# Keys of two inputs from one moving operand, and attention tiles in the halves of the context rows

## The chip, the cores and the metric

The kernel runs on one core of a Trainium2 chip. The metric is device time in microseconds of one execution; the median of three runs of the kernel before is 1750.83 us (1750.73 to 1752.44). A profiled execution on the same chip gives the trace.

## What is computed

One layer of a block over 256 latent tokens and 256 context tokens of width 2048, all in float32. Both inputs are normalized and modulated; the latent one goes through one large input projection, the context only through its key and value columns. Three branches follow: a convolution of 31 taps, a gating unit with a layer norm and a mixing matmul over tokens, and an attention of 16 heads whose keys are the latent tokens of a window and all of the context. The branches are gated, summed and projected, and a squared-ReLU MLP of width 8192 ends the layer.

```python
hl = modulate(rms_norm(xl, norm1_g[l]), mod_l[0], mod_l[1])
hc = modulate(rms_norm(xc, norm1_g[l]), mod_c[0], mod_c[1])
zl = hl @ w_in[l] + b_in[l]
zkv = hc @ w_in[l, :, K_OFF:G_OFF] + b_in[l, K_OFF:G_OFF]
kc, vc = split_heads(zkv[..., :NA_DIM]), split_heads(zkv[..., NA_DIM:])
y_na_l = neighbourhood_attention(q, k, v, kc, vc, na_rpb[l])
xl = xl + mod_l[2][:, None, :] * mixer_output(zl, y_na_l, *branch_params)
hl2 = modulate(rms_norm(xl, norm2_g[l]), mod_l[3], mod_l[4])
xl = xl + mod_l[5][:, None, :] * sq_relu_ffn(hl2, w_ff1[l], b_ff1[l], w_ff2[l], b_ff2[l])
```

## The kernel before

Every float32 product is made of three: a value is split into a high part (`hi`) and the rest (`lo`), and hi x hi, hi x lo and lo x hi are summed in PSUM. Weights come in as `raw` tiles of 128 x 1024 on the SP queue (ring of 8); ScalarE casts each to `whi` (L102) and VectorE subtracts to get `wlo` (L105), each in a ring of four, so that a `wlo` of a step can be written only when TensorE is done with the one four steps earlier. One such tile feeds about twelve matmuls. Rows of the inputs are transposed once and kept as `h`: 128 features by 512, the high parts of 256 tokens and then the low parts, two feature tiles in one unit of the shared pool, and each input has its own eight units (`hl[v][kt]`).

The shared pool (`unit`, `HEAP` = 27 units of 4 KB a partition) serves nearly all larger tiles of the program, one after another; a tile gets the slot of one whose last reader is done, and its first writer waits for that reader. A scheduler orders the instructions of each engine beforehand, from the order of the code and from when it takes slots and inputs to be ready; on the chip each engine runs its list in that order and waits where it must.

The stages: the modulation vectors and the first rows (to about 30 us); five blocks of keys and values over both inputs (to some 240 us), whose feature tiles are `BLOCKS`; the queries, and the attention beside the convolution's projections; the gating unit's projections (to about 540 us); three branch projections with their gates (to some 940 us); the output projection and the MLP.

Of these the change touches:

- the keys in `kv_block` (`kfn`): for each key tile `nt` and each input, `mm_w` runs per feature tile one matmul of 512 columns (L203, weight high part x rows high and low) and one of 256 (L205, weight low part x rows high, added onto the second half of the bank). The two halves of the bank are then joined and added to `kT`: in block 0 by an ACT step with the bias (L435) and a DVE add (L436), in the other blocks by an ACT copy (L438), a DVE add (L439) and a POOL add (L440), for each of the two inputs. The values `vb` (L212 to L215, `mm_x`) are added by one DVE step of 128 x 512 (L456).
- the attention: `qT` for queries (units of two tiles), `kh` and `kl` for the parts of a key tile (`att_keys`, L547 to L552), `oT` for the outputs (L617 and on) have units of their own; `S` (L583, L584) are scores, `pT` (L606) the transposed weights.
- by the pool, what comes later. The convolution reads its input `uT` with 248 steps on DVE, spread over the code (`conv_taps`, L689 and L692). The gating unit (`sgu_var`) squares its rows into a pool tile `svq` on ACT (L856), for the sum alone; then come L858 (DVE), L859 (POOL), `sgu_norm` (L862, L863 on DVE) and `sgu_mix`, eight pairs of matmuls (L871). Beside them the first branch runs with its gates (L897, L907). The steps of the modulation of later stages (L944, L946 on DVE, `mcol` L975) go between all of these.

## Time and profile before

| | us |
|---|---|
| median of three runs | 1750.83 |
| profiled execution | 1752.01 |
| its span | 1750.2 |
| PE busy | 1719.4 (98%) |
| DVE busy | 1333.6 (76%) |
| ACT busy | 874.6 (50%) |
| POOL busy | 127.3 (7%) |

PE is the engine of the matmuls, DVE VectorE, ACT ScalarE, POOL GpSimd. A busy time is the time in which at least one instruction runs; matmuls overlap at their ends, so that the distance of two starts tells what one costs, and its own duration is longer. The profile was taken from one execution, whose own time is 1.2 us above the median.

### The profile page before, as it was taken

How to read it: one execution, taken by the hardware profiler on the slowest of the kernel's cores; microseconds unless marked ns; L12 is line 12 of the kernel's file. 1: busy time of each engine (PE TensorE's matmuls, PEld its weight loads, DVE VectorE, ACT ScalarE, POOL GpSimd, SP SyncE). 2: the span in 40 equal slices, each digit the busy share in tenths (PEclk: the TensorE clock that was granted, in tenths of full speed). 3: DMA queues.
4: the chain of work that ended last, by engine and by line, in shares of the span. 5: the costliest groups of instructions: out<-in, count | busy, mean ns of one | idle time of the engine just before them, and what ended most of it. 6: DMA issues, size and time to landing. Idle time of an engine off the chain costs nothing.

```text
span 1750.2 us, 24238 instructions
## 1 busy us (share of the span) xinstructions
PE 1719.4 (98%) x8849; PEld 1426.7 (82%) x8849; DVE 1333.6 (76%) x2088; ACT 874.6 (50%) x1298; POOL 127.3 (7%) x179
## 2 busy tenths in 40 slices
PE   6999999999999999999999999999999999999997
PEld 4667878788888888788888888888888888888886
DVE  4655789799999987997889878756885576666665
ACT  4433427986545444564444565434543455335543
POOL 2222230110000010200000010000000000000000
PEclk9999999999999999999999999999999999999999
DMA  9898578657667778898898977867886776666552
GB/s 322 283 322 272 151 221 255 185 141 214 198 191 225 226 235 279 271 314 297 291 300 296 316 238 251 259 194 225 276 270 195 220 241 191 204 193 190 187 195 79
DMA packets 266969, 411.87 MB, mean 235 GB/s; under 512 B 13182, under 2 KB 128050, under 8 KB 266850
## 3 DMA queue, kind: packets, MB, share of 16 engines
q1 hardware_dynamic: 259410, 391.21, 68.9%
q0 software_dynamic: 6864, 18.07, 4.4%
q8 instruction: 69, 1.13, 0.3%
q10 hardware_dynamic: 576, 1.05, 0.2%
q14 instruction: 50, 0.41, 0.1%
HBM read 408.18 MB, written 2.10 MB: 234 GB/s over the span
## 4 chain that ended last, share of the span: by engine, by line
PE 79%; DVE 1%; ACT 1%; issue 0%; POOL 0%; POOLq 0%; DVEq 0%
PE bk L203 18%; PE bk L212 16%; PE bk L213 16%; PE bk L215 16%; PE bk L205 9%; PE o L617 1%; PE pT L606 1%; PE S L584 0%; PE S L583 0%; DVE wlo L105 0%; PE mrow L965 0%; PE mix L871 0%; PE mT L920 0%; ACT whi L102 0%; PE x1T L1138 0%
## 5 line engine op out<-in xcount | busy, mean ns | idle before, releaser
L102 ACT CAST whi<-raw 128x1024 fp32r<-128x1024 f32 x544 | 571.3, 1052 | 663.8 <-PE bk L213 430.3
L105 DVE TENSOR_TENSOR wlo<-raw,whi 128x1024 fp32r<-128x1024 f32 x544 | 670.3, 1234 | 285.2 <-ACT whi L102 274.9
L203 PE MATMUL bk<-h,whi 128*128 128x512 f32 x1536 | 395.1, 394 | 0.2 <-DVE h L1190 0.2
L203 PEld LDWEIGHTS bk<-h,whi 128*128 128x128 f32 x1536 | 273.8, 189 | 50.7 <-issue 2.7
L205 PEld LDWEIGHTS bk<-h,wlo 128*128 128x128 f32 x1536 | 216.0, 190 | 19.4
L205 PE MATMUL bk<-h,wlo 128*128 128x256 f32 x1536 | 221.7, 282 | 0.0
L213 PE MATMUL bk<-whi,g 128*128 128x512 f32 (+1 forms) x516 | 199.7, 387 | 0.0
L212 PE MATMUL bk<-whi,g 128*128 128x512 f32 (+1 forms) x516 | 199.7, 387 | 0.0
L946 DVE SCALAR_TENSOR_TENSOR ga<-raw,cst,ga 128x512 f32<-128x512 f32 x240 | 186.4, 777 | 2.1
L212 PE MATMUL bk<-whi,h 128*128 128x512 f32 x448 | 175.4, 392 | 0.0
L213 PE MATMUL bk<-whi,h 128*128 128x512 f32 x448 | 174.4, 389 | 0.0
L215 PE MATMUL bk<-wlo,g 128*128 128x512 f32 (+1 forms) x516 | 139.3, 387 | 0.0
L215 PE MATMUL bk<-wlo,h 128*128 128x512 f32 x448 | 122.2, 389 | 0.0
L212 PEld LDWEIGHTS bk<-whi,g 128*128 128x128 f32 x516 | 96.9, 188 | 19.7
L213 PEld LDWEIGHTS bk<-whi,g 128*128 128x128 f32 x516 | 96.9, 188 | 19.7
L215 PEld LDWEIGHTS bk<-wlo,g 128*128 128x128 f32 x516 | 96.5, 188 | 19.8
L692 DVE SCALAR_TENSOR_TENSOR cT<-uT,wcT,cT 128x249 f32<-128x249 f32 (+14 forms) x240 | 103.6, 476 | 0.6
L215 PEld LDWEIGHTS bk<-wlo,h 128*128 128x128 f32 x448 | 84.1, 188 | 17.5
L213 PEld LDWEIGHTS bk<-whi,h 128*128 128x128 f32 x448 | 84.1, 188 | 17.1
L212 PEld LDWEIGHTS bk<-whi,h 128*128 128x128 f32 x448 | 84.1, 188 | 17.0
L203 PE MATMUL k<-h,whi 128*128 128x512 f32 x256 | 69.2, 404 | 4.9 <-DVE t L439 2.5
L440 POOL TENSOR_TENSOR kT<-kT,t 128x256 f32<-128x256 f32 x64 | 52.6, 845 | 139.8 <-DVE t L439 139.5
(276 smaller groups left out, 1975.5 us busy)
## 6 DMA issues: line engine op xcount, KB each, us to landing
raw<-in_w_ff_dram SPq DMA_DIRECT2D x256, 512.0 KB, 4.4
raw<-in_w_in_dram SPq DMA_DIRECT2D x208, 512.0 KB, 4.7
raw<-in_w_mod_dram SPq DMA_DIRECT2D x192, 512.0 KB, 5.4
raw<-in_w_o_dram SPq DMA_DIRECT2D x32, 512.0 KB, 5.5
raw<-in_w_na_out_dram SPq DMA_DIRECT2D x16, 512.0 KB, 4.5
raw<-in_w_sgu_out_dram SPq DMA_DIRECT2D x16, 512.0 KB, 5.6
raw<-in_w_conv_out_dram SPq DMA_DIRECT2D x16, 512.0 KB, 5.4
bias<-in_na_rpb_dram POOLq DMA_DIRECT2D x16, 192.0 KB, 4.9
```

Source lines behind the costliest of these rows:

```text
L102: nc.scalar.copy(hv, rv)
L105: self.low[j] = nc.vector.tensor_tensor(lv, rv, hv.bitcast(F32), ALU.subtract)
L203: PE.matmul(bk, lhsT=hi[:, j, c0 : c0 + P], rhs=xhl, start=start, stop=False)
L205: PE.matmul(bk[:, T:], lhsT=lo[:, j, c0 : c0 + P], rhs=xhl[:, :T], start=False, stop=stop)
L212: PE.matmul(bk, lhsT=xhl[:, t * P : (t + 1) * P], rhs=hi, start=start, stop=False)
L213: PE.matmul(bk, lhsT=xhl[:, T + t * P : T + (t + 1) * P], rhs=hi, start=False, stop=False)
L215: last["mm"] = PE.matmul(bk, lhsT=xhl[:, t * P : (t + 1) * P], rhs=lo, start=False, stop=stop)
L440: GP.tensor_tensor(d, d, f, ALU.add)
L606: PE.transpose(b[:, kt * T + t * P : kt * T + (t + 1) * P], s[:, t, (2 * g + kt) * P : (2 * g + kt + 1) * P], ident)
L617: PE.matmul(b[64 * j : 64 * j + 64, :T], lhsT=vN[kt][:, h * 64 : h * 64 + 64], rhs=pts[j][:, kt], start=kt == 0, stop=kt == 3)
L692: V.scalar_tensor_tensor(a[:, lo:hi], u[:, lo + d : hi + d], wj, a[:, lo:hi], ALU.mult, ALU.add)
L946: V.scalar_tensor_tensor(a[0], raw[:, r], sc, a[0], ALU.mult, ALU.add)
```

## The change

The unit of a feature tile now holds both inputs: the latent rows in its first half, the context rows in its second (`hl[kt][:, v]`), sixteen units either way. In blocks 1 to 4 a key matmul reads the high parts of both inputs at once, or the low parts of both (`mm_both`): two pieces of 256 columns, one from each half. All three products go to the same bank, 256 columns for each input, and one DVE add of 128 x 512 brings it to `kT`. Block 0, where the two inputs come at different times, runs three matmuls of 256 columns per input (`mm_one`), and ACT adds the bias on the way to `kT`. Once the values have used the context rows, their halves take the queries and the attention outputs (`spare_half`, tiles 0 to 7) and the key parts (tiles 8 to 15, by turns); `qT`, `kh`, `kl` and `oT` need no units any more.

```diff
--- before.py
+++ after.py
@@ -303,7 +303,7 @@
 
     m1A = cp.tile([P, NK, 2], F32, name="m1A")
     m1B = cp.tile([P, NK, 2], F32, name="m1B")
-    hl = [[None] * NK, [None] * NK]
+    hl = [None] * NK
     kT = [None] * 8
     vN = [None] * 4
 
@@ -397,11 +397,9 @@
                     tps = aux("hT")
                     for t in range(2):
                         PE.transpose(tps[:, t * P : (t + 1) * P], nat[v][kt // 4][:, t, (kt % 4) * P : (kt % 4 + 1) * P], ident)
-                    if kt % 2 == 0:
-                        hl[v][kt] = unit([P, 2, 512], F32R, "h")
-                    else:
-                        hl[v][kt] = hl[v][kt - 1]
-                    dst = hl[v][kt][:, kt % 2]
+                    if hl[kt] is None:
+                        hl[kt] = unit([P, 2, 512], F32R, "h")
+                    dst = hl[kt][:, v]
                     sA, sB = m1A[:, kt, v : v + 1], m1B[:, kt, v : v + 1]
                     last["hi"] = S.activation(dst[:, :T], tps[:, :T], AF.Identity, bias=sB, scale=sA)
                     f = tmp(256, "hf")
@@ -411,7 +409,28 @@
         return steps, post
 
     def H(v, kt):
-        return hl[v][kt][:, kt % 2]
+        return hl[kt][:, v]
+
+    def spare_half(kt):
+
+        return hl[kt][:, 1]
+
+    def mm_both(b, hi, lo, c0, kts):
+
+        bv = b.rearrange("p (v t) -> p v t", v=2)
+        for j, kt in enumerate(kts):
+            PE.matmul(bv, lhsT=hi[:, j, c0 : c0 + P], rhs=hl[kt][:, :, :T], start=j == 0, stop=False)
+            PE.matmul(bv, lhsT=hi[:, j, c0 : c0 + P], rhs=hl[kt][:, :, T:], start=False, stop=False)
+        for j, kt in enumerate(kts):
+            PE.matmul(bv, lhsT=lo[:, j, c0 : c0 + P], rhs=hl[kt][:, :, :T], start=False, stop=j == len(kts) - 1)
+
+    def mm_one(todo):
+
+        for bk, hi, lo, j, c0, xhl, start, stop in todo:
+            PE.matmul(bk[:, :T], lhsT=hi[:, j, c0 : c0 + P], rhs=xhl[:, :T], start=start, stop=False)
+            PE.matmul(bk[:, :T], lhsT=hi[:, j, c0 : c0 + P], rhs=xhl[:, T:], start=False, stop=False)
+        for bk, hi, lo, j, c0, xhl, start, stop in todo:
+            PE.matmul(bk[:, :T], lhsT=lo[:, j, c0 : c0 + P], rhs=xhl[:, :T], start=False, stop=stop)
 
     def kv_block(bi):
         k0, nk = BLOCKS[bi]
@@ -421,23 +440,23 @@
         def kfn(p, vs=(0, 1)):
             def fn(*ws):
                 hi, lo = ws[0]
-                n = kc // P if bi == 0 and p == 0 and vs == (0,) else 1
+                if bi:
+                    for i in range(kc // P):
+                        nt = kc // P * p + i
+                        b = bank("k")
+                        mm_both(b, hi, lo, i * P, range(k0, k0 + nk))
+                        d = kT[nt][:, nt % 2]
+                        V.tensor_tensor(d, d, b, ALU.add)
+                    return
+                n = kc // P if p == 0 and vs == (0,) else 1
                 for i0 in range(0, kc // P, n):
                     bs = {(i, v): bank("k") for i in range(i0, i0 + n) for v in vs}
-                    mm_w([(b, hi, lo, j, i * P, H(v, k0 + j), j == 0, j == nk - 1) for (i, v), b in bs.items() for j in range(nk)])
+                    mm_one([(b, hi, lo, j, i * P, H(v, k0 + j), j == 0, j == nk - 1) for (i, v), b in bs.items() for j in range(nk)])
                     for (i, v), b in bs.items():
                         nt = kc // P * p + i
                         if kT[nt] is None:
                             kT[nt] = kT[nt ^ 1] = unit([P, 2, 512], name="kT")
-                        d = kT[nt][:, nt % 2, v * T : (v + 1) * T]
-                        f = tmp()
-                        if bi == 0:
-                            S.activation(f, b[:, T:], AF.Identity, bias=par["k"][:, nt : nt + 1])
-                            V.tensor_tensor(d, b[:, :T], f, ALU.add)
-                        else:
-                            S.copy(f, b[:, T:])
-                            V.tensor_tensor(f, b[:, :T], f, ALU.add)
-                            GP.tensor_tensor(d, d, f, ALU.add)
+                        S.activation(kT[nt][:, nt % 2, v * T : (v + 1) * T], b[:, :T], AF.Identity, bias=par["k"][:, nt : nt + 1])
             return fn
 
         def vfn(cb, vs=(0, 1)):
@@ -523,9 +542,7 @@
             V.scalar_tensor_tensor(g.rearrange("p (r c) -> p r c", c=64)[:, :, ::-1],
                                    b[:, :T].rearrange("p (r c) -> p r c", c=64), 0.125,
                                    f.rearrange("p (r c) -> p r c", c=64), ALU.mult, ALU.add)
-            if i == 0:
-                qT[nt] = qT[nt + 1] = unit([P, 2, 2, T], F32R, "qT")
-            q = qT[nt][:, i]
+            q = qT[nt] = spare_half(nt).rearrange("p (h t) -> p h t", h=2)
             up, dn = slice(0, 64), slice(64, P)
             S.copy(q[up, 0], g[up])
             S.copy(q[dn, 1], g[dn])
@@ -539,17 +556,18 @@
 
         bias_tile(nt)
         k = kT[nt][:, nt % 2]
-        hi = unit([P, 2, 512], F32R, "kh")
-        lo = unit([P, 2, 512], F32R, "kl")
+        at = 8 + 4 * (nt % 2)
+        hi = [spare_half(at + r) for r in range(2)]
+        lo = [spare_half(at + 2 + r) for r in range(2)]
         kW[nt] = hi, lo
         half = [slice(0, 64), slice(64, P)]
         for r in range(2):
-            S.copy(hi[half[r], r], k[half[r]])
-            S.copy(hi[half[1 - r], r], k[half[r]])
+            S.copy(hi[r][half[r]], k[half[r]])
+            S.copy(hi[r][half[1 - r]], k[half[r]])
         for r in range(2):
-            V.tensor_tensor(lo[half[r], r], k[half[r]], hi[half[r], r].bitcast(F32), ALU.subtract)
+            V.tensor_tensor(lo[r][half[r]], k[half[r]], hi[r][half[r]].bitcast(F32), ALU.subtract)
         for r in range(2):
-            S.copy(lo[half[1 - r], r], lo[half[r], r].bitcast(F32))
+            S.copy(lo[r][half[1 - r]], lo[r][half[r]].bitcast(F32))
 
     mask = cp.tile([P, 64], F32, name="mask")
     GP.memset(mask, 0.0)
@@ -579,9 +597,9 @@
         for t in range(2):
             b = aux("S")
             hi, lo = kW[nt]
-            q = qT[nt][:, nt % 2, h % 2, t * P : (t + 1) * P]
-            PE.matmul(b, lhsT=q, rhs=hi[:, h % 2], start=True, stop=False)
-            PE.matmul(b, lhsT=q, rhs=lo[:, h % 2], start=False, stop=True)
+            q = qT[nt][:, h % 2, t * P : (t + 1) * P]
+            PE.matmul(b, lhsT=q, rhs=hi[h % 2], start=True, stop=False)
+            PE.matmul(b, lhsT=q, rhs=lo[h % 2], start=False, stop=True)
             V.tensor_tensor_reduce(s[:, t, :T], b[:, :T], bt[nt][:, h % 2, (2 - 2 * t) * 64 : (6 - 2 * t) * 64],
                                    scale=-1.0, scalar=BIG, op0=ALU.add, op1=ALU.min, accum_out=mx[:, 2 * t : 2 * t + 1])
             V.tensor_tensor_reduce(s[:, t, T:], b[:, T:], zero, scale=-1.0, scalar=mx[:, 2 * t : 2 * t + 1],
@@ -615,9 +633,7 @@
             for j in range(2):
                 h = 2 * nt + j
                 PE.matmul(b[64 * j : 64 * j + 64, :T], lhsT=vN[kt][:, h * 64 : h * 64 + 64], rhs=pts[j][:, kt], start=kt == 0, stop=kt == 3)
-        if nt % 2 == 0:
-            oT[nt] = oT[nt + 1] = unit([P, 2, 512], F32R, "oT")
-        o = oT[nt][:, nt % 2]
+        o = oT[nt] = spare_half(nt)
         bv = b[:, :T].rearrange("p (r c) -> p r c", c=64)[:, :, ::-1]
         S.copy(o[:, :T].rearrange("p (r c) -> p r c", c=64), bv)
         V.tensor_tensor(o[:, T:].rearrange("p (r c) -> p r c", c=64), bv,
@@ -1092,7 +1108,7 @@
                 V.tensor_tensor(xb[cb][:, t], xb[cb][:, t], bo, ALU.add)
         return fn
 
-    branches = [(2, w_na_out[0], lambda kt: oT[kt][:, kt % 2]), (1, w_sgu_out[0], lambda kt: sgT[kt][:, kt % 2]),
+    branches = [(2, w_na_out[0], lambda kt: oT[kt]), (1, w_sgu_out[0], lambda kt: sgT[kt][:, kt % 2]),
                 (0, w_conv_out[0], lambda kt: cvT[kt][:, kt % 2])]
     for n, (br, w, xs) in enumerate(branches):
         for cb in range(4):
```

Line numbers behind the first of these places are higher in the changed kernel: the keys' matmuls are L422, L423, L425 and, in block 0, L430, L431, L433, their add is L449, the values' add L475, and from the attention on every line is 16 further (L856 becomes L872, L871 becomes L887).

TensorE in block 1, two key tiles in four banks (`k`), with `h_648` latent and `h_663` context rows, before:

```order
L203 MATMUL k_719<-h_648,whi_616 128x512 x2
L203 MATMUL k_720<-h_663,whi_616 128x512 x2
L205 MATMUL k_719<-h_648,wlo_617 128x256 x2
L205 MATMUL k_720<-h_663,wlo_617 128x256 x2
L203 MATMUL k_737<-h_648,whi_616 128x512 x2
L203 MATMUL k_738<-h_663,whi_616 128x512 x2
L205 MATMUL k_737<-h_648,wlo_617 128x256 x2
L205 MATMUL k_738<-h_663,wlo_617 128x256 x2
```

and in the changed program, a key tile and the start of another, each in one bank, with `h_648` and `h_656` two feature tiles of both inputs:

```order
L422 MATMUL k_717<-h_648,whi_616 128x512
L423 MATMUL k_717<-h_648,whi_616 128x512
L422 MATMUL k_717<-h_656,whi_616 128x512
L423 MATMUL k_717<-h_656,whi_616 128x512
L425 MATMUL k_717<-h_648,wlo_617 128x512
L425 MATMUL k_717<-h_656,wlo_617 128x512
L422 MATMUL k_725<-h_648,whi_616 128x512
L423 MATMUL k_725<-h_648,whi_616 128x512
```

The matmuls of two inputs into two banks have become matmuls over both into one.

DVE in the gating unit; `cT` and `uT` are the convolution's sum and input, `sv` the unit's rows, `th`, `bk` and `m` the first branch's gate, bank and product. Before:

```order
L858 TENSOR_SCALAR sgu_var<-sgu_var 128x2
L692 SCALAR_TENSOR_TENSOR cT_4347<-uT_4346,wcT,cT_4347 128x243
L862 SCALAR_TENSOR_TENSOR sv_5082<-sv_5082,sgu_var,lg_5101 128x1024
L105 TENSOR_TENSOR wlo_5567<-raw_5564,whi_5566 128x1024
L105 TENSOR_TENSOR wlo_5605<-raw_5602,whi_5604 128x1024
L863 TENSOR_TENSOR sv_5082<-sv_5082,lb_5103 128x1024
L862 SCALAR_TENSOR_TENSOR sv_5084<-sv_5084,sgu_var,lg_5101 128x1024
L105 TENSOR_TENSOR wlo_5626<-raw_5623,whi_5625 128x1024
L897 TENSOR_TENSOR th_5635<-bk_5475,gb_5467 128x512
```

and in the changed program:

```order
L105 TENSOR_TENSOR wlo_5695<-raw_5692,whi_5694 128x1024
L708 SCALAR_TENSOR_TENSOR cT_3955<-uT_3954,wcT,cT_3955 128x242
L708 SCALAR_TENSOR_TENSOR cT_3955<-uT_3954,wcT,cT_3955 128x241
L874 TENSOR_SCALAR sgu_var<-sgu_var 128x2
L923 SCALAR_TENSOR_TENSOR m_5351<-th_5243,bk_5271 128x512
L923 SCALAR_TENSOR_TENSOR m_5351<-th_5252,bk_5272 128x512
L878 SCALAR_TENSOR_TENSOR sv_4690<-sv_4690,sgu_var,lg_4709 128x1024
L878 SCALAR_TENSOR_TENSOR sv_4692<-sv_4692,sgu_var,lg_4709 128x1024
L879 TENSOR_TENSOR sv_4690<-sv_4690,lb_4711 128x1024
L879 TENSOR_TENSOR sv_4692<-sv_4692,lb_4711 128x1024
```

The sgu steps stood among taps and weight steps; now they stand in one piece, behind the last tap, and behind two gating products.

ACT's squares `svq` (L856), on which the first of these DVE steps waits, came right behind the centering of `sv`; they now come some twenty casts later, and the first of them waits for the last tap on DVE, since its tile has the slot of a `uT`.

TensorE at the first mixing matmuls (`mix`; `ws` the mixing weights), before:

```order
L215 MATMUL bk_5765<-wlo_5762,h_986 128x512 x2
L215 MATMUL bk_5766<-wlo_5762,h_986 128x512 x2
L871 MATMUL mix_5855<-ws_5088,sv_5082 128x128
L871 MATMUL mix_5855<-ws_5088,sv_5084 128x128
L212 MATMUL bk_5765<-whi_5784,h_1510 128x512
```

and in the changed program:

```order
L212 MATMUL bk_5699<-whi_5603,h_299 128x512
L213 MATMUL bk_5699<-whi_5603,h_299 128x512
L215 MATMUL bk_5698<-wlo_5604,h_291 128x512
L215 MATMUL bk_5698<-wlo_5604,h_299 128x512
L215 MATMUL bk_5699<-wlo_5604,h_291 128x512
L887 MATMUL mix_5463<-ws_4696,sv_4690 128x128
L887 MATMUL mix_5511<-ws_4696,sv_4690 128x128
L887 MATMUL mix_5568<-ws_4696,sv_4690 128x128
L887 MATMUL mix_5630<-ws_4696,sv_4690 128x128
L215 MATMUL bk_5699<-wlo_5604,h_299 128x512
L887 MATMUL mix_5463<-ws_4696,sv_4692 128x128
L887 MATMUL mix_5511<-ws_4696,sv_4692 128x128
```

The first mix stood by itself between weight steps; now four of them, and the same four for the second half of the rows, stand a weight matmul apart, and the first waits for L879, the second group for the second L879.

## Rows read from the trace of the kernel before

**Rows 1.** The page: busy us, share of the span, instructions of each engine.

```profile
PE 1719.4 (98%) x8849; PEld 1426.7 (82%) x8849; DVE 1333.6 (76%) x2088; ACT 874.6 (50%) x1298; POOL 127.3 (7%) x179
```

**Rows 2.** Windows: stretch, its us, busy us of PE, PEld, DVE, ACT, POOL, granted clock.

```profile
220.00:240.00 20.00, 16.09 (x86) 13.40 (x85) 19.90 (x28) 6.55 (x20) 11.92 (x14) 1.00 0.80 246
240.00:300.00 60.00, 59.04 (x321) 50.43 (x320) 51.29 (x91) 32.60 (x58) 4.04 (x5) 1.00 0.81 244
300.00:340.00 40.00, 38.57 (x236) 31.75 (x235) 33.59 (x81) 38.72 (x79) 5.48 (x6) 1.00 0.72 198
540.00:640.00 100.00, 100.00 (x458) 83.35 (x457) 99.11 (x168) 46.97 (x56) 11.06 (x13) 1.00 0.70 225
```

**Rows 3.** Waits of PE from 27 to 340 us: total us, times, longest us.

```profile
PE k L203 <- DVE t L439: 2.5, 2, 1.7
...
PE mcol L975 <- DVE ga L946: 1.8, 2, 1.4
PE S L584 <- ACT kl L552: 0.8, 1, 0.8
```

**Rows 4.** Timeline of PE from 173 to 176 us: start, us, instructions.

```profile
173.12 1.12 PE L205 MATMUL k<-h,wlo 128*128 128x256 f32 x8
174.07 2.00 PE L203 MATMUL k<-h,whi 128*128 128x512 f32 x8
175.91 0.28 PE L205 MATMUL k<-h,wlo 128*128 128x256 f32 x1
```

**Rows 5.** Groups by line from 20 to 260 us: count, busy us, mean ns, idle before.

```profile
L203 PE MATMUL k<-h,whi 128*128 128x512 f32 x256 | 69.2, 404 | 4.9 <-DVE t L439 2.5 <-ACT whi L102 1.9 <-DVE h L409 0.4
...
L439 DVE TENSOR_TENSOR t<-k,t 128x256 f32<-128x256 f32 x64 | 25.0, 417 | 24.6 <-ACT t L438 24.2
...
L456 DVE TENSOR_TENSOR vN<-vN,vb 128x512 f32<-128x512 f32 x32 | 21.4, 682 | 16.5 <-PE vb L215 16.4
```

**Rows 6.** Timeline of DVE and POOL from 221 us, and the group of L946, 200 to 240.

```profile
221.11 0.75 DVE L946 SCALAR_TENSOR_TENSOR ga<-raw,cst,ga 128x512 f32<-128x512 f32 x1
...
223.41 0.73 POOL L440 TENSOR_TENSOR kT<-kT,t 128x256 f32<-128x256 f32 x1 [2.88 <-DVE t L439]
223.58 1.11 DVE L946 SCALAR_TENSOR_TENSOR ga<-raw,cst,ga 128x512 f32<-128x512 f32 x1
...
L946 DVE SCALAR_TENSOR_TENSOR ga<-raw,cst,ga 128x512 f32<-128x512 f32 x16 | 16.1, 1010 | 0.1
```

**Rows 7.** Timelines of the gating unit from 541 us, and of DVE at the last tap.

```profile
542.54 1.06 ACT L856 ACTIVATE svq<-sv 128x1024 f32<-128x1024 f32 x1
...
544.54 0.18 ACT L856 ACTIVATION_READ_ACCUMULATOR svq<-sv 128x1 f32 x1
...
546.19 1.28 DVE L862 SCALAR_TENSOR_TENSOR sv<-sv,sgu_var,lg 128x1024 f32<-128x1024 f32 x1 [0.61 <-POOL sgu_var L859]
...
549.66 1.22 DVE L863 TENSOR_TENSOR sv<-sv,lb 128x1024 f32<-128x1024 f32 x1
...
574.23 0.60 PE L871 MATMUL mix<-ws,sv 128*128 128x128 f32 x4
...
635.31 0.68 DVE L907 SCALAR_TENSOR_TENSOR m<-th,bk 128x512 f32<-128x512 f32 x1
635.91 1.22 DVE L105 TENSOR_TENSOR wlo<-raw,whi 128x1024 fp32r<-128x1024 f32 x1
637.04 0.47 DVE L692 SCALAR_TENSOR_TENSOR cT<-uT,wcT,cT 128x241 f32<-128x241 f32 x1
637.42 1.22 DVE L105 TENSOR_TENSOR wlo<-raw,whi 128x1024 fp32r<-128x1024 f32 x1
```

**Rows 8.** Windows at the first weight step, granted clock behind POOL's column.

```profile
28.00:30.00 2.00, 0.15 (x1) 0.18 (x2) 1.63 (x5) 2.00 (x4) 0.00 (x0) 1.00 1.05 385
30.00:32.00 2.00, 2.00 (x7) 1.53 (x8) 2.00 (x3) 1.39 (x3) 0.00 (x0) 0.63 1.05 387
32.00:34.00 2.00, 2.00 (x9) 1.81 (x8) 1.44 (x2) 0.50 (x2) 0.00 (x0) 0.52 1.05 383
```

## The prediction

> **What bounds the kernel now.** I read the page's busy shares first: the matmul engine is busy for 1719.4 of 1750.2 us [rows 1], so at most about 31 us of the span are idle on it, and everything this change can gain lies there or in the number and length of matmuls. The table by stretch comes next: 220 to 240 us holds 16.09 us of matmul in 20, beside a VectorE that is busy for 19.90, while from 540 to 640 us both PE and DVE are full (100.00 and 99.11 of 100) [rows 2]. So PE sets the pace, and DVE is the engine behind it in two places: at the end of the key and value blocks, and in the stretch with the convolution taps. The list of PE's waits says what ends them: 2.5 us on the DVE add that joins halves of a key (L439), 1.8 us on an accumulation for the modulation (L946), 0.8 us on the low key part in the attention (L552) [rows 3].
>
> **Part 1, the key matmuls.** Per key tile and weight row the kernel runs two matmuls of 512 columns and two of 256; the changed one runs three of 512. Both move 1536 columns. In the timeline eight 256-column matmuls start 0.95 us before the next group, so 119 ns each, and eight of 512 take 1.84 us, 230 ns each [rows 4]. Before: 2 x 230 + 2 x 119 = 698 ns; after: 3 x 230 = 690. There are 8 tiles x 14 rows = 112 of these in blocks 1 to 4: -0.9 us. Block 0 takes six of 256 columns for two of 512 and two of 256, 714 for 698, 16 times: +0.3 us. Together -0.6 us. No row shows a matmul whose moving operand is two pieces of 256 columns a tile apart. It can't well cost more than two matmuls of 256, 238 ns, so 336 x 8 ns = +2.7 us is one end; the other is 0, since the matmul reads the same number of rows of the same memory. I take 0 and keep 2.7 for the range.
>
> **Part 2, joining the halves.** Removed are 64 copies on ACT (L438), 64 DVE adds of 417 ns (L439; the row of the window holds 25.0 us of busy time, since they overlap a little), 64 POOL adds (L440), and 16 DVE adds in block 0 (L436). Added are 32 DVE adds of 128x512 from a bank. The trace has one of that shape, L456, at 682 ns [rows 5]: 64 x 417 - 32 x 682 ns = 4.9 us less on DVE in blocks 1 to 4, of which a quarter, 1.2 us, in the last one. A second relief: an L946 step takes 0.75 us alone and 1.11 us where a POOL add runs beside it, and the 16 of them from 200 to 240 us average 1010 ns, 4.2 us over the undisturbed sum [rows 6]. All of this is work beside the matmuls, and it is worth something only where PE waits for it, 220 to 240 us, whose idle time is 20 - 16.09 = 3.9 us [rows 2]. The two longest waits there end with L439, queued behind L946 steps [rows 3, 6]; with 4.2 + 1.2 = 5.4 us less on DVE in that stretch they should nearly vanish. I take -3.5 us, of 0 to -3.9. The Trainium skill ("SBUF — State Buffer", "SBUF: two separate sides") says that the pair of ports which VectorE shares with GpSimd is locked for a whole instruction, so that a DVE operation with two SBUF inputs is fully blocked; the 0.36 us added to L946 is half of the POOL add's 0.73 us, as if the two had begun at different moments. By that rule the relief could be twice as large, and the term would be -3.9 instead of -3.5.
>
> **Part 3, the attention.** Key parts, queries and outputs go to halves that are there already, so that an attention step waits less for a free tile, and the keys no longer wait for the POOL adds. From 240 to 340 us the idle time of PE is 0.96 + 1.43 us by the table, and the one of them that the edit takes away by name is the wait of 0.8 us on the low key part [rows 2, 3]. The chains behind the others (scores to softmax to transposes) stay, but start from less crowded engines. I take -1.9 us, between 0 and the whole, -2.4. Sum of gains: -0.6 - 3.5 - 1.9 = **-6.0 us**, bounds +2.1 (a slower operand, nothing gained else) and -6.9.
>
> **Part 4, where the freed tiles went.** This is the term on the other side. The context rows used to give back their eight tiles after the last value block, and the attention outputs theirs after the first branch; now all sixteen tiles of rows stay until the last gate matmul. The 27 slots of the shared pool are dealt out by release, so late tiles get other slots. The order shows where that bites: the tile for the squares of the gating branch (svq, L856) now gets the slot of the second convolution input, which is in use until the last of the 248 taps. ACT's two L856 move down by twenty weight casts, to behind the last tap, DVE's L858, L862 and L863 with them, and the first four mixing matmuls (L871) move some 110 main matmuls, about 24 us, down PE's order. In the kernel before, L856 began at 542.54 us, the first L863 was done at 550.9 and the first mix ran at 574.23, far behind; the last tap is at 637.04 [rows 7].
>
> In the new order there is no slack. The last two taps on DVE stand behind one wlo step, which waits until PE has finished the matmuls of the step four earlier. From that matmul on, the way is: wlo 1.13 us (635.91 to 637.04), two taps at 0.38 (637.04 to 637.42) 0.8 us, both L856 with their reads 2.2 us (542.54 to 544.72), L858 at most 0.1, then the first of two gating products L907 0.6 us (635.31 to 635.91) [rows 7]. PE's very next matmul group needs the bank that this product frees: PE stands for 4.8 us. The second L907 0.6 us hides behind four matmuls. Then L862 twice and L863 once, at about 1.2 us each (1.28 and 1.22 with their overlap), 3.6 us; POOL's power step between L858 and L862 hides behind the two L907 (before, the whole way from L856's end to L862 was 1.47 us, 544.72 to 546.19). So the first mix is ready 4.8 + 0.6 + 3.6 = 9.0 us after that matmul. PE has eleven matmuls of 230 ns to do, 2.5 us, up to 7.3: 1.7 us more. The second row half is another L863 later, 0.45 us after four mixes and a matmul, and the next mix waits for a DVE step behind the delayed wlo, some 0.3. With about 0.25 us for the four handovers: 4.8 + 1.7 + 0.45 + 0.3 + 0.25 = **+7.5 us**, bounds 6.5 and 9 (DVE, full as before, comes late to that wlo step). Queued behind the waiting L856 on ACT are casts for three steps later; PE has three steps in store after the mixes, so nothing more comes of it. The cover that is gone is the slack of some 20 us.
>
> **Part 5, the clock.** At 28 to 30 us PE was idle for 1.85 of 2 us, and the granted clock was 0.63 and 0.52 in the next two stretches of 2 us, where 1 is 2.4 and 0.5 is 1.2 GHz [rows 8]. The loss is some 1.7 us (0.37 x 2 + 0.48 x 2). The waits of 1.7 and 1.4 us at 220 to 240 us cost no clock (1.00) [rows 2, 3]. A stand of 4.8 us followed by another of 1.7 is longer than all of these, so I add **+1.7 us**; bounds 0 and 3.4 (twice). The Trainium skill ("TensorE: Matmul & The Clock Gate", "What's actually happening") knows two levels, the lower one after idling; this is the rule that speaks against the change, and without it the sum would be 1.7 us lower.
>
> **The sum.** -6.0 + 7.5 + 1.7 = +3.2 us. The profiled execution is 1752.0 us (span 1750.2 and 1.8 around it), 1.2 over the median 1750.83. So 1752.0 + 3.2 - 1.2 = **1754.0 us**. A measurement of this kernel tells 0.2%, 3.5 us, from no change: below 1747.3 is faster, above 1754.3 slower. The forecast lies at the edge.
>
> **The rivals.** (a) The stall comes, the clock holds: 1752.3 us. For it: waits of up to 1.7 us left the clock alone; against it: 28 us. (b) Slower clearly: the same place, but DVE is late. It has all taps to finish before the squares, in a stretch where it is full; if it lags PE by 2 us when it reaches that wlo step, the stand grows by as much, and with a moving operand that costs its 2.7 us the time is 1754 + 2 to 4.7 = 1756 to 1758.7. It decides as soon as DVE's last taps end later than PE's step four earlier. Against it, by a bare margin: from the wlo step where the order of before and after part, 72 taps at 0.38, 23 wlo steps at 1.13 and some 8 us of gate and modulation work make 61 us, and the 23 steps of twelve matmuls last 23 x 12 x 0.23 = 63 us on PE [rows 4, 7]. (c) Faster: PE's rows hide small waits as busy time. The 256 key matmuls of 512 columns average 404 ns [rows 5], where one of an undisturbed group takes 2.00 - 7 x 0.23 = 0.39 [rows 4]; 256 x 14 ns = 3.6 us of short waits would sit in that and go too. With those, the clock held and the stand at its lower bound: -6.9 - 3.6 + 6.5 = -4.0 us, 1746.8. (d) The stand doesn't appear, because the mixes are not where I take them or the slot is freed sooner: 1750.8 - 6.0 = 1744.8. The order is fixed in the program, and the wait on the last tap is in it, so I give this little.
>
> **Chances.** The forecast 0.48 (own range 1751.5 to 1757, split evenly around 1754.3), (a) 0.20, (b) 0.16, (c) 0.10, (d) 0.06. Faster: (d) and most of (c), 0.14; slower: half the forecast and (b), 0.40; the rest, 0.46, same. The range leaves out (d) and the worst of (b): 1746.5 to 1758.
>
> **What would show it.** In the changed trace: key matmuls at 230 ns from start to start, two-piece operand or not; 220 to 240 us with PE at 19 or more of 20 and no wait on the key add; a wait of PE of about 5 us ended by L923 (old L907) near 600 us and one of 1.5 to 2 ended by L879 (old L863), ACT's squares right after the last tap; a granted clock under 1 behind it. It is wrong if PE runs through 590 to 610 us without a wait, if the key stage keeps its idle time, or if the key matmuls start further apart than 235 ns.

## The result

| | us |
|---|---|
| before, median of 4 runs | 1750.78 |
| changed, median of 4 runs | 1759.88 (1759.72 to 1761.11) |
| ratio | 1.0052, interval 1.004 to 1.0064 |
| span of the profiled execution | 1759.3 |
| PE busy | 1720.0 |
| forecast | 1754.0, range 1746.5 to 1758.0 |

The kernel is slower by 9.1 us, on the side that the forecast leaned to and above its range. To see where, I took the same matmul of the program (one of the `bk` matmuls, counted from the first) in both traces and subtracted its starts. Below zero the changed kernel is ahead; I call that its lead. Both traces are of executions 1.2 us above their medians, so that the 9.07 us at the end are the 9.1 of the medians.

| time in the trace of before, us | place | changed less before, us |
|---|---|---|
| 257 | first query matmul | -5.75 |
| 307 | attention | -7.2 |
| 430 | attention over | -2.17 |
| 592 | before the mixes | -2.9 |
| 621 | after the mixes | +7.25 |
| 924 | last branch | +7.5 |
| 948 | behind its gates | +9.05 |
| 1712 | MLP, to the end | +9.07 |

So there are gains up to 307 us and three losses behind them: 5.75 us won by the end of the keys and 1.45 more by 307 us, then some 5 us of lead lost in the attention, 9.4 us from 430 to 621 us, at the mixes, and 1.55 us at the last gates. The step from -2.17 to -2.9 before the mixes is mostly no gain but work that moved: in that time the kernel before runs three groups of mixing matmuls, from 574.23 us on, and the changed kernel runs all of its mixes behind 605 us. So the mixes are counted from 430 us.

The windows of the changed kernel answer to [rows 2] (columns as there; the last three are clock, DMA share and GB/s):

```profile
220.00:240.00 20.00, 19.95 (x91) 16.26 (x90) 15.03 (x24) 5.03 (x12) 0.00 (x0) 1.00 0.78 257
240.00:300.00 60.00, 60.00 (x336) 52.00 (x335) 57.42 (x103) 42.22 (x77) 3.72 (x3) 1.00 0.82 251
300.00:340.00 40.00, 35.59 (x222) 29.43 (x222) 29.35 (x76) 35.16 (x70) 6.11 (x7) 1.00 0.61 167
...
540.00:640.00 100.00, 93.43 (x417) 76.72 (x416) 92.81 (x160) 42.05 (x51) 11.10 (x12) 0.97 0.66 207
```

220 to 240 us, which held 16.09 us of matmul, now holds 19.95, with DVE at 15.03 instead of 19.90. But 300 to 340 fell from 38.57 to 35.59, and 540 to 640 from 100.00 to 93.43 at a clock of 0.97. The waits of PE name the places (total us, times, longest):

```profile
PE bk L212 <- DVE m L923: 6.5, 1, 6.5
PE o L635 <- DVE mx L605: 3.3, 5, 1.0
...
PE mT L936 <- DVE m L926: 1.2, 2, 0.9
PE S L601 <- DVE mx L605: 1.2, 1, 1.2
...
PE k L430 <- ACT h L404: 0.7, 1, 0.7
PE k L431 <- DVE h L407: 0.6, 1, 0.6
```

The waits on the key add [rows 3] are gone. In their place stand 6.5 us on the first gating product (L923), 3.3 and 1.2 us on L605, a step of the scores, and 1.2 us on the last gates' sum (mT, on L926). The wait of 1.9 us on the first weight cast has become two, of 0.7 and 0.6 us, on the first rows.

**The keys.** In the timeline of PE two key tiles stand like this (start, duration, instruction):

```profile
170.53 0.39 PE L422 MATMUL k<-h,whi 128*128 128x512 f32 x1
...
172.34 1.07 PE L425 MATMUL k<-h,wlo 128*128 128x512 f32 x4
173.25 0.39 PE L422 MATMUL k<-h,whi 128*128 128x512 f32 x1
```

and, for comparison, matmuls of the values (PE from 236 to 240 us), whose moving operand is one piece of 512 columns:

```profile
236.53 1.07 PE L215 MATMUL vb<-wlo,h 128*128 128x512 f32 x4
237.44 0.39 PE L212 MATMUL vb<-whi,h 128*128 128x512 f32 x1
```

Twelve key matmuls, all of two pieces, start within 173.25 - 170.53 = 2.72 us, 227 ns each; four of one piece take 237.44 - 236.53 = 0.91, the same 227. The two pieces cost nothing here. The groups of the window from 20 to 260 us answer to [rows 5, 6]:

```profile
L449 DVE TENSOR_TENSOR kT<-kT,k 128x512 f32<-128x512 f32 x32 | 21.9, 684 | 37.5 <-PE k L425 37.5
...
L962 DVE SCALAR_TENSOR_TENSOR ga<-raw,cst,ga 128x512 f32<-128x512 f32 x28 | 20.9, 745 | 0.2
```

The add of both inputs takes 684 ns (682 expected), and L962, the old L946, is back at 745 ns, where 16 of them averaged 1010 [rows 6]: no POOL adds run beside them any more. The Trainium skill ("SBUF — State Buffer", "SBUF: two separate sides") says that of a DVE operation with two SBUF inputs and a GpSimd operation that reads SBUF only one has the shared pair of ports at a time; the trace agrees, with 1.11 us beside a POOL add [rows 6] and 745 ns without.

**The mixes.** The timeline from 592 to 606 us (engines mixed):

```profile
593.31 2.51 DVE L708 SCALAR_TENSOR_TENSOR cT<-uT,wcT,cT 128x247 f32<-128x247 f32 x5
...
594.01 0.61 PE L215 MATMUL bk<-wlo,h 128*128 128x512 f32 x2
594.21 1.05 ACT L102 CAST whi<-raw 128x1024 fp32r<-128x1024 f32 x1 [2.07 <-PE bk L213]
595.73 1.22 DVE L105 TENSOR_TENSOR wlo<-raw,whi 128x1024 fp32r<-128x1024 f32 x1
596.87 0.97 DVE L708 SCALAR_TENSOR_TENSOR cT<-uT,wcT,cT 128x242 f32<-128x242 f32 x2
...
597.87 1.06 ACT L872 ACTIVATE svq<-sv 128x1024 f32<-128x1024 f32 x1 [2.62 <-DVE cT L708]
...
600.23 0.17 DVE L874 TENSOR_SCALAR sgu_var<-sgu_var 128x2 f32<-128x2 f32 x1 [2.39 <-ACT svq L872]
600.31 1.27 DVE L923 SCALAR_TENSOR_TENSOR m<-th,bk 128x512 f32<-128x512 f32 x2
...
601.14 0.77 PE L212 MATMUL bk<-whi,h 128*128 128x512 f32 x1 [6.51 <-DVE m L923]
...
601.50 2.47 DVE L878 SCALAR_TENSOR_TENSOR sv<-sv,sgu_var,lg 128x1024 f32<-128x1024 f32 x2
601.70 0.63 PE L213 MATMUL bk<-whi,h 128*128 128x512 f32 x1
...
603.90 2.35 DVE L879 TENSOR_TENSOR sv<-sv,lb 128x1024 f32<-128x1024 f32 x2
...
604.69 1.22 PE L215 MATMUL bk<-wlo,h 128*128 128x512 f32 x3
...
605.75 0.49 PE L887 MATMUL mix<-ws,sv 128*128 128x128 f32 x3
```

This is the chain of the forecast, piece by piece: the wlo step, two taps, the two squares, L874, the first L923, and PE's next group starts at its end, 601.14. What differs most is its first link. PE's last matmuls end at 594.62 (594.01 + 0.61), and the wlo step starts 1.1 us later. The forecast let it start at once. But the step also reads the tile that ACT casts to `whi`, and that cast runs from 594.21 to 595.26. So 0.64 us of the 1.1 belong to the cast, and only the other 0.47, up to 595.73, to the five taps that DVE still has to do. With somewhat longer taps, squares and first product, PE stands for 6.5 us, not 4.8.

The clock in the same place (columns as [rows 8]):

```profile
598.00:600.00 2.00, 0.00 (x0) 0.00 (x0) 0.00 (x0) 1.97 (x3) 0.00 (x0) 0.66 0.76 245
600.00:602.00 2.00, 0.86 (x2) 0.80 (x3) 1.77 (x4) 0.20 (x2) 0.83 (x2) 0.50 0.04 15
602.00:604.00 2.00, 2.00 (x6) 1.52 (x6) 2.00 (x3) 0.00 (x0) 0.47 (x1) 0.50 0.26 80
604.00:606.00 2.00, 2.00 (x9) 1.59 (x8) 2.00 (x2) 1.05 (x1) 0.00 (x0) 0.63 0.15 51
```

It fell while PE was idle, and of the eleven matmuls up to the first mix most then take 0.43 us apiece instead of 0.23 (601.70 to 604.69 is seven of them); all eleven take 4.6 us instead of 2.5. That fills the time in which L878 and the first L879 run, so the second stand of the forecast is not seen.

### The profile page after: what moved, and what is told of

It reads as the page before. It is cut to its first block, busy times and chain, and to the rows that moved or that the text cites. A ratio compares the mean times of both kernels' runs of the same rounds, so it can differ in the third digit from the quotient of the medians.

```text
span 1759.3 us, 23816 instructions
## 1 busy us (share of the span) xinstructions
PE 1720.0 (98%) x8769; PEld 1421.7 (81%) x8769; DVE 1313.5 (75%) x2040; ACT 853.0 (48%) x1234; POOL 76.7 (4%) x115
## 4 chain that ended last, share of the span: by engine, by line
PE 88%; DVE 4%; DMA 3%; issue 3%; ACT 1%; POOL 1%; SPq 0%; POOLq 0%; DVEq 0%; ACTq 0%
PE bk L203 18%; PE bk L212 16%; PE bk L213 16%; PE bk L215 16%; PE bk L205 9%; DMA bias<-in_na_rpb_dram 2%; PE gemv L356 2%; PE vb L212 1%; PE vb L213 1%; PE vb L215 1%; DVE wlo L105 1%; DMA raw<-in_w_in_dram 1%; PE k L422 1%; PE k L423 1%; PE k L425 1%
## 5 line engine op out<-in xcount | busy, mean ns | idle before, releaser
L212 PE MATMUL bk<-whi,h 128*128 128x512 f32 x512 | 201.6, 394 | 6.6 <-DVE m L923 6.5
L213 PE MATMUL bk<-whi,h 128*128 128x512 f32 x512 | 200.4, 391 | 0.0
L962 DVE SCALAR_TENSOR_TENSOR ga<-raw,cst,ga 128x512 f32<-128x512 f32 x240 | 182.2, 759 | 2.2
L215 PE MATMUL bk<-wlo,h 128*128 128x512 f32 x512 | 140.7, 390 | 0.0
L212 PEld LDWEIGHTS bk<-whi,h 128*128 128x128 f32 x512 | 96.7, 189 | 27.4 <-ACT svq L872 6.9
L215 PEld LDWEIGHTS bk<-wlo,h 128*128 128x128 f32 x512 | 96.5, 189 | 20.1
L213 PEld LDWEIGHTS bk<-whi,h 128*128 128x128 f32 x512 | 96.7, 189 | 19.7
L708 DVE SCALAR_TENSOR_TENSOR cT<-uT,wcT,cT 128x244 f32<-128x244 f32 (+14 forms) x240 | 101.9, 468 | 0.6
L212 PE MATMUL vb<-whi,h 128*128 128x512 f32 x128 | 51.0, 400 | 0.1
L212 PE MATMUL bk<-whi,mhl 128*128 128x512 f32 (+1 forms) x132 | 50.9, 388 | 0.0
```

The costliest lines, as they stand in the source:

```text
L212: PE.matmul(bk, lhsT=xhl[:, t * P : (t + 1) * P], rhs=hi, start=start, stop=False)
L213: PE.matmul(bk, lhsT=xhl[:, T + t * P : T + (t + 1) * P], rhs=hi, start=False, stop=False)
L215: last["mm"] = PE.matmul(bk, lhsT=xhl[:, t * P : (t + 1) * P], rhs=lo, start=False, stop=stop)
L708: V.scalar_tensor_tensor(a[:, lo:hi], u[:, lo + d : hi + d], wj, a[:, lo:hi], ALU.mult, ALU.add)
L962: V.scalar_tensor_tensor(a[0], raw[:, r], sc, a[0], ALU.mult, ALU.add)
```

## The experiments

Each was timed beside the kernel before on its own chip: 1750.96 us for svq_tmp, bias_early, both_slots and old_keys, 1751.27 for heap28, heap29, before_r6 and no_bias_read, 1751.16 for the others. Where two runs from different groups are compared, 0.3 us of the difference can be the chip's.

**svq_tmp.** Only the place and the type (bf16) of a tile that nobody reads:

```diff
-        sq = unit([P, 1024], name="svq")
+        sq = tmp(512, "svq").bitcast(mybir.dt.bfloat16)
```

> The changed kernel with one edit: the squares of the gating unit (svq, written and never read, only their sum counts) go to a small tile in bf16 outside the shared pool, so that they wait for no tap. Theory (pool slots): the stand of PE at 594 us and the slower clock behind it go, 10.5 us by the offsets of the two traces; 1759.9 - 10.5 = 1749.4 us, bias waits in the attention and the wait at 945 us stay. Rival (DVE is too full in the stretch with the taps, so PE would stand there anyway): 1755 us or more, with PE waiting for a wlo step or a tap between 560 and 640 us.

Measured 1751.42 (1750.73 to 1752.77), 8.5 us under the changed kernel. The lead in its trace is -1.36 from 430 us to 667, without a step at the mixes; the wait of 6.5 us is not among those of PE from 430 to 940 us:

```profile
PE mT L936 <- DVE m L926: 0.9, 1, 0.9
PE mrow L981 <- ACT ah L978: 0.8, 1, 0.8
PE mrow L981 <- DVE ah L979: 0.2, 1, 0.2
```

So the slot of this one tile cost 8.5 us by the medians and 9.4 by the leads from 430 to 621 us (its lead at 430 us was 0.8 smaller in this execution). DVE is as busy there as before (99.03 of 100 us from 540 to 640), so a full DVE by itself does not make PE stand.

**bias_early.**

```diff
+            if h % 2 == 0 and h + 2 < HEADS:
+                bias_tile(h // 2 + 1)
             if h < HEADS:
                 att_scores(h)
```

(and no longer in `att_keys`, but for the first).

> The changed kernel with one edit: the bias tile of a pair of heads is taken one attention step earlier in the code, before the score tile, so that it no longer takes the slot of the bias tile before it. Theory (pool slots): DVE no longer waits for the bias transfer (7.5 us in three waits now) and PE not for L605; 4.8 us of the lead that PE had at 300 us stay, 1755 us. Rival (the attention is slower because key parts, queries and outputs share halves): no change within 1 us of 1759.9.

Measured 1779.53, 20 us slower. **both_slots**, both edits:

> Both of these edits at once. Theory: the gains add, 1759.9 - 10.5 - 4.8 = 1744.6 us, below the kernel before (1750.8) by about 6, with only the wait at 945 us (1.6 us) left. Rival (each takes work from where the other needs it): 1749 or more.

Measured 1768.53. Both miss, in the same way. The wait for the bias is indeed short now, but the scores end much later. The first line is of the changed kernel, the second of bias_early (32 score steps with the bias: min/median/max ns, first and last start):

```profile
L603 DVE CUSTOM_DVE_ANT_0 s<-S,bias x32: 405/418/425, 278.1 to 408.0; 128x256 f32<-128x256 f32 x32
```

```profile
L604 DVE CUSTOM_DVE_ANT_0 s<-S,bias x32: 407/421/425, 276.7 to 474.6; 128x256 f32<-128x256 f32 x32
```

A bias tile taken earlier takes the slot that some other tile had. In bias_early POOL stands for 105.9 us before it fills the seventh of the eight bias tiles, at 447.94 us, just when output matmuls (L636) end that PE ran only at 444 us, behind the convolution's projections. Here a slot was not had by asking earlier. The edit tested the place of the request, not the price of the wait.

**old_keys.** `kfn` of the kernel before (four matmuls, copy, two adds), all else as changed.

> The changed kernel with the keys of the kernel before: four matmuls per pair, a bank for each input, ACT copy, DVE add, POOL add. Queries, outputs and key parts stay in the halves. Theory (the keys are a gain, the halves a loss): the lead of 5.75 us at the first query matmul is gone, 1765.6 us, and the stands at 594 us and in the attention are as in the changed kernel. Rival (the gain before 240 us came from the freed tiles or the first block, not from the joined matmuls): within 2 us of 1759.9.

Measured 1767.35, 7.5 us over the changed kernel (5.7 were expected). Its stretch from 220 to 240 us is that of the kernel before:

```profile
220.00:240.00 20.00, 16.08 (x86) 13.26 (x86) 19.86 (x30) 8.40 (x23) 11.70 (x12) 1.00 0.72 222
```

The losses are in it too: 7.6 us are lost from 307 to 430 us, in the attention, and 9.0 from there to 621 us. So the keys by themselves gain 7.5 us, and the rest of the change loses some 16, 1.9 of them before the first query matmul.

**heap28** and **heap29**: more pool slots, paid by the ring of weight tiles.

```diff
-RBUF = 8
-HEAP = 27
+RBUF = 7     (6 in heap29)
+HEAP = 28    (29)
```

> The changed kernel with 28 pool slots instead of 27, paid by a ring of 7 instead of 8 raw weight tiles. By the program the squares (svq) no longer get the slot of a uT, and of the last five bias tiles three no longer follow the one before in its slot. Theory (one slot too few): no stand at 594 us, -10.5 us against the changed kernel, and about half of the 4.8 us of the attention: 1747 us, if the shorter ring costs nothing. Rival (the squares and bias tiles don't matter, or the ring is what feeds PE): 1757 us or more, with PE or ACT waiting for raw transfers.

> The changed kernel with 29 pool slots, paid by a ring of 6 raw tiles. No bias tile follows another that was just used, the squares wait for no tap. Theory: -10.5 and -4.8 us: 1744.6 us, one or two more if the first x tile, which also comes earlier, takes the 1.6 us at 945 us away. Rival (ring): more than 1750, with waits on raw transfers in the stretches where the DMA engines are near full (40 to 140 and 640 to 1000 us).

and **before_r6**, the price of the shorter ring:

> The kernel before with a ring of 6 instead of 8 raw weight tiles and nothing else: the price of the shorter ring that pays for two pool slots. If PE has enough steps in store: within 1 us of 1750.8. If the ring feeds PE where the DMA engines are near full: 1753 or more.

Measured 1750.49 (1747.71 to 1752.56), 1760.39 and, for the kernel before with the ring of 6, 1762.26: the ring costs 11 us there. Its casts wait much longer for weights (ACT's waits from 20 to 1740 us, the kernel before first, then before_r6):

```profile
ACT whi L102 <- DMA raw<-in_w_in_dram: 17.3, 9, 7.0
```

```profile
ACT whi L102 <- DMA raw<-in_w_in_dram: 50.0, 28, 7.1
...
ACT whi L102 <- DMA raw<-in_w_o_dram: 27.7, 16, 3.9
```

The trace of heap28 has neither the stand at the mixes nor the waits on L605, so one slot is enough for both; what its ring of 7 cost was not run by itself. With the price of the ring of 6 taken off, heap29 would stand near 1749; the sum is not clean, so the slots had to be paid otherwise.

**no_bias_read.** On top of svq_tmp, the scores add `zero` instead of `bt[nt]`.

> The changed kernel with the squares outside the pool (as svq_tmp, 1751.4 us), in which the scores add a tile of zeros instead of the bias tile: the neighbourhood bias and its mask are left out of the result, the bias is still loaded. It prices the wait for the bias alone. Theory (the late bias costs the attention 4.8 us): 1746.6 us. Rival (the attention waits for the softmax chain itself): 1751 us.

Measured 1747.10 (1745.89 to 1748.07), 4.3 us under svq_tmp. (The two traces lie 6 us apart, since the one of svq_tmp is a long execution and this one a short one; the medians are the price.) The lead stays: -7.7 at 307 us, -7.9 at 430. PE's waits from 250 to 430 us are

```profile
PE mcol L991 <- DVE ga L962: 1.6, 1, 1.6
PE o L635 <- DVE mx L605: 0.2, 1, 0.2
```

The late bias is thus the price of the attention. Why it is late shows in the waits of the changed kernel: of POOL, which fills the tile with the mask and issues its load, and of DVE, which needs it, both from 290 to 420 us.

```profile
POOL bias L585 <- DVE mx L603: 71.2, 5, 16.3
```

```profile
DVE s L603 <- DMA bias<-in_na_rpb_dram: 7.5, 3, 3.6
```

Five bias tiles get the slot of the bias tile before them: POOL may begin only when the score steps of the previous pair of heads, its last readers, are done (L603), and the next pair's scores stand until the transfer lands. In the kernel before, POOL waited there for a key copy (L548), transposes, a score matmul and a query step, and DVE not at all for a bias.

**slots28.** One slot more without touching the ring:

```diff
-HEAP = 27
+HEAP = 28
-tag=f"tmp{n}", bufs=6 if n == 256 else 7     (and 7 for a1, ga)
+tag=f"tmp{n}", bufs=6 if n == 256 else 5
```

> The changed kernel with 28 pool slots instead of 27, paid by 5 instead of 7 small tiles of 128x512; the ring of 8 raw tiles stays, and the squares stay in the pool. By the program the squares take no uT slot, and three bias tiles instead of five follow one another in a slot. Theory (one slot too few): the stand at 594 us goes (-8.5 as the squares alone gave) and most of the attention's 4.3: 1747 us. Rival (it was not the slot but the place of the squares in the code, or five small tiles hold something up): 1752 us or more.

Measured 1747.73, 0.9981 (0.9972 to 0.999) of the kernel before: 12.1 us under the changed kernel by one slot of 4 KB. DVE's wait for the bias from 290 to 420 us is down from 7.5 to

```profile
DVE s L603 <- DMA bias<-in_na_rpb_dram: 0.2, 1, 0.2
```

Its lead is -6.5 at 257 us, -8.7 from 430 to 784 us; it loses 5.8 of that between 840 and 860 us, where PE waits 2.0 us for a row of the modulation (mrow, on L978) and its clock falls again (0.83). (The trace is of the slowest of its eleven executions, 1749.62 us.) That row is late because of an x tile of the output projection: DVE stands on its transfer for 3.3 us, and behind it in DVE's list is the step L962 that ACT's L978 waits for (the window, then the timeline):

```profile
840.00:860.00 20.00, 17.70 (x64) 13.64 (x64) 13.20 (x17) 6.82 (x8) 1.10 (x2) 0.83 0.69 221
```

```profile
841.96 0.69 DVE L1108 TENSOR_TENSOR xb<-xb,bo 128x512 f32<-128x512 f32 x1 [3.28 <-DMA xb<-in_x_dram]
842.57 0.75 DVE L962 SCALAR_TENSOR_TENSOR ga<-raw,cst,ga 128x512 f32<-128x512 f32 x1
...
843.35 0.62 ACT L978 CAST ah<-ga 128x512 fp32r<-128x512 f32 x1 [3.87 <-DVE ga L962]
```

heap28, the other kernel with 28 slots, has it smaller (DVE 1.9 us on the x tile, PE 0.7 us on L978).

**xb_late** (`XB` = 9 instead of 6, on svq_tmp) and **bias_last** (the bias tile taken at the end of an attention step, on svq_tmp):

> The changed kernel with the squares outside the pool (svq_tmp, 1751.4 us), and the x tiles of the output projection loaded and added three weight steps later in the code, so that DVE no longer stands on their transfer ahead of the last gate products. Theory (PE's wait at 945 us is DVE's wait for the x tile): no such wait, 1.2 us less, 1750.2. Rival (DVE is late there by its own work): 1751.4 and the wait on L926 stays.

> The changed kernel with the squares outside the pool, and the bias tile taken at the end of an attention step, after the tile of transposed weights, so that most bias tiles follow a score or weight tile in its slot and not the bias tile before. Theory (the chain of bias tiles in one slot is what makes the bias late): DVE's wait for the bias falls under 2 us and 3 of the 4.3 us come back, 1748.4. Rival (any slot comes free too late while only three or so are in play): the wait stays, 1751 or more.

xb_late: 1750.61, 0.8 under svq_tmp; the intervals of the two against the kernel before overlap, but its trace has no wait on the last gates any more, and its lead stands at -1.3 at 924 and 948 us, where the changed kernel loses 1.55. So PE's wait goes when the x steps move away from the last gates. In the changed kernel (860 to 945 us) DVE waits for three transfers of x tiles, and POOL, which issues them, stood on a gate matmul that still read its rows:

```profile
DVE xb L1108 <- DMA xb<-in_x_dram: 6.9, 3, 4.2
```

```profile
POOL xb L1102 <- PE bk L215: 28.9, 1, 28.9
```

The kernel before has no such wait of DVE. But in xb_late DVE still waits 6.8 us for x tiles; that it is this wait, and not the place of the x steps ahead of the gate products, that delays PE is not shown.

bias_last: 1755.60, 4 us slower than svq_tmp and not faster (its executions spread from 1751.79 to 1757.91, and the profiled one is among the short ones). In its trace the bias wait of DVE only fell from 5.4 to 5.0 us, and the score steps wait 3.9 us for transposes, so the expectation failed: here a slot that followed another tile came no earlier than one that followed a bias tile. What it is worth to be rid of the bias wait is known from no_bias_read; by moving the request I did not get it.

**slots28_all.** slots28, svq_tmp and `XB` = 9 together.

> A version that should beat both: 28 slots for 27 with 5 small tiles for 7, the squares outside the pool, the x tiles three steps later. Theory: the key part's gain of some 6 us without the three losses, 1745 us, 0.3% under the kernel before. Rival (five small tiles or the later x tiles cost as much): 1750.

Measured 1744.55 (1743.6 to 1745.11), 0.9964 (0.995 to 0.9977) of the kernel before, 6.6 us faster, and 15.3 under the changed kernel. Its lead is -9.7 from 430 to 784 us and -8.4 at the end, and the loss of slots28 between 840 and 860 us is not in it. The kernel before with the same three remedies was not run, so how much of the 6.6 us the change itself earns is not shown. The windows (columns as [rows 2]):

```profile
220.00:240.00 20.00, 20.00 (x92) 16.55 (x91) 14.88 (x23) 5.59 (x12) 0.00 (x0) 1.00 0.72 236
...
300.00:340.00 40.00, 38.73 (x247) 31.86 (x246) 30.88 (x74) 38.37 (x78) 6.67 (x8) 1.00 0.74 192
...
540.00:640.00 100.00, 100.00 (x459) 83.35 (x458) 95.59 (x155) 45.45 (x54) 12.07 (x13) 1.00 0.71 229
```

## Why the prediction was wrong

- **Key matmuls** (-0.6): right on the open point. 227 ns each from start to start, 0 for the two pieces, not 2.7. The -0.6 itself is not seen apart from the next term.
- **Joining** (-3.5): right in kind, too small. The idle time of 220 to 240 us went from 3.9 to 0.05 us, and the lead at the first query matmul is 5.75; old_keys prices the keys at 7.5. By the matmuls of the values the lead is 2.4 us at 37 us, 0.5 at 201 and 5.7 at 235, so most of what is left was won in the last stretch, as forecast; where the early lead went I did not follow. At the start, two waits of 0.7 and 0.6 us at 27 to 29 us take the place of the idle time of 28 to 30 us, and the clock stays at 1.00, where it fell before [rows 8]; the changed kernel's windows there:

```profile
28.00:30.00 2.00, 1.30 (x8) 1.10 (x9) 1.96 (x5) 2.00 (x4) 0.00 (x0) 1.00 1.05 386
30.00:32.00 2.00, 2.00 (x19) 1.94 (x17) 2.00 (x3) 1.63 (x5) 0.00 (x0) 1.00 1.05 387
```

- **Attention** (-1.9): wrong, and this is the step that failed. It said that "an attention step waits less for a free tile". It counted the units that the halves make unnecessary and not the eight that the context rows no longer give back. The one wait that it named, 0.8 us on the low key part, did go; it is in the 1.45 us won up to 307 us. But between 307 and 430 us 5 us of lead were lost, because the attention's steps waited more, and for a tile: five bias tiles had to follow each other in a slot (no_bias_read: 4.3 us by the medians). Over both, the term measured +3.6. I had followed the slots for the gating unit only; the same list for the bias tiles would have shown the chain.
- **The mixes** (+7.5, and +1.7 for the clock): the mechanism and the place were right, and 9.2 became 9.4 by the leads. That the sums agree so well is partly luck. The first stand was 6.5 for 4.8, while the second one (1.7) never showed, since the slow clock (2.1 for eleven matmuls) filled its time: the two were added where they overlap. Of the 1.1 us by which the wlo step came late, DVE's own lag, of which rival (b) warned, is only 0.47; the other 0.64 are the ACT cast, a link that the forecast's chain left out. The clock fell, which rival (a) denied.
- **x tiles**: 1.55 us at the last gates that were not in the sum. At least one x tile waits for a gate matmul to be done with its rows; the rows now hold all sixteen units until the last gates, where eight had come free.
- The sum of what was seen: -5.75 + 3.6 (257 to 430 us) + 9.4 (430 to 621) + 0.25 (621 to 924, not followed) + 1.55 = 9.05. The forecast's +3.2 misses it by 5.9. The attention alone is 5.5 off, +3.6 for -1.9; the x tiles and the small rest add 1.8, and 1.65 more won at the keys (5.75 for 4.1) hide almost as much.

## What to carry to other kernels

Where all larger tiles share one pool of slots, a change that keeps some of them longer has a price that lies anywhere behind it, in any tile that is dealt another slot: list, for each tile taken while the kept ones live, whose last reader it now waits for, and do so for all of them. A tile that nobody reads should not stand in such a pool. The remedy that worked here was one more slot, from small tiles of which fewer were enough; its 12.1 us are more than the keys' 7.5. Asking for the tile earlier, or later, made it worse.

## What the runs showed of the hardware

Matmuls of 512 columns from two pieces of 256 a tile half apart started every 227 ns, like those from a single piece. PE's clock fell from its higher level to its lower one in the stand of 6.5 us, while PE was still idle (0.66 in the window from 598 us), and stayed at 0.50 for some 4 us of work; it fell in slots28 too, with a stand of 2.0 us (0.83 from 840 to 860 us), and the two waits of 0.7 and 0.6 us at 27 to 29 us left it at 1.00. A ring of 6 weight tiles of 512 KB instead of 8 cost 11 us in the kernel before, although PE's own list of waits there names a transfer for only 0.8 us.
